# Bounds, orders and the gate tiles' load moved, and every third low part of the gate build given to GpSimd, in a hybrid SSD, attention and PEER block

## The chip, the cores and the metric

The kernel runs on one core of one Trainium2 chip. The metric is the device time of one execution in microseconds (us). The kernel before takes 1569.84 us, the median of three runs (1566.93, 1569.84 and 1572.42). The engines are TensorE (PE; its weight loads are shown as PEld), VectorE (DVE), ScalarE (ACT), GpSimd (POOL) and SyncE (SP, which only issues transfers here).

## The reference

One post-norm layer on x of 512 tokens by 1024, float32, in three parts:

```python
h = layer_norm(x)
proj = h @ w_in                                   # SSM columns | MLA columns
y = concat([ssd(16 heads), mla(8 heads)]) @ w_out # the mixer
h = layer_norm(alpha * h + y)
# PEER: 8 heads, product keys
q = (h @ w_query).reshape(T, 8, 2, 128)
s = einsum('thkd,hknd->thkn', q, sub_keys)
sv, si = top_k(s, 16)                             # per half
top_s, top_pos = top_k(sums of the two halves, 16)
gate = softmax(top_s)                             # expert = i * 128 + j, 16384 experts
act = gelu(einsum('td,thkd->thk', h, u_table[expert]))
ffn = einsum('thk,thkd->td', gate * act, v_table[expert])
out = layer_norm(alpha * h + ffn)
```

## The kernel before, in words

**Stages.** The times in brackets are those of the profiled execution. First come the first layer norm, the projections, the SSM heads and the attention (0 to about 310 us), then the output projection w_out with the second layer norm, block by block of 128 tokens (to about 394). Then comes PEER. The first 384 tokens (NT) are treated densely: the 16384 experts are 128 chunks of 128, and for every chunk the kernel computes act = gelu(U chunk times x) for tokens 0 to 351 (NU); the gates are spread into a dense matrix of expert by token; and the V chunks are multiplied with gate times act and summed up in six PSUM banks (va). Tokens 352 to 383 (UG, 32 of them) get their act from gathered rows of u (`ug_dots`, L1303 to L1321), and the last 128 tokens are done wholly with gathered rows of u and v during the V stage (`gather`).

**U chunks.** A U chunk is 24 matmuls of 128 by 352 (L77 to L79 in `mm3`): high part times high part of x, high times low, low times high, all in f16. `u_halves` (L1519) does one chunk in two halves. The f16 parts come from `Stream`: a raw f32 chunk is loaded by SyncE's queue; `square` (L126) sums its squares on ScalarE; `bound` (L129 to L138) adds these over the partitions with one matmul of 128 by 2 (usq against ones, into any PSUM bank that it is given) and three tiny ScalarE operations make of that a power of two as the scale (us) and its inverse (ui); `his` casts the scaled chunk to f16 on ScalarE (L171); and `splits` makes the low part. On VectorE the low part is one operation with the scale in it (L193, SCALAR_TENSOR_TENSOR, raw times scale less the high part). On GpSimd it is a plain subtraction (L191), and ScalarE first scales the raw chunk in place (L170). Which engine does it is told by `lo_on`: VectorE in routing and in the gate build, GpSimd in the query stage.

**Order.** The program is written out by hand in one order, and each engine runs its own instructions of it strictly in that order. `get` prepares items two ahead; a bound covers two chunks up to chunk 72 (FB), one from there on; `tick` and `bounds` decide by the number of the current chunk which squares and bounds are issued. The 54 first U chunks (LEAD) are spread over the query stage (408 to 517), routing (517 to 565) and the gate build; the others alternate with V chunks in the V stage (from about 760). In the query stage, `w_query_fm` does one query block of 128 columns, `sub_scores` its scores, and `stage1` the top 16 on VectorE. Head 3's result for the last block's tokens is copied to memory by three transfers on ScalarE's queue (r3d). In `routes` VectorE turns positions into expert numbers and ScalarE does the exponential of the softmax.

**Gate build.** `build_g` runs 48 steps. In each, VectorE makes a one-hot of the expert's second digit (`oj`, L1402) and the product of the other digits' one-hots with the gate (`gi`, L1405) for 8 tokens, both f16 with all inputs in SBUF; TensorE multiplies them in 16 small matmuls into two `pw` banks (L1432), ScalarE evicts these to `stg` (L1434), and every fourth step `stg` goes to memory (gs0 for the first two tiles of four chunks, gsp for the others). In the same step there is a dot of one gathered row (L1307 on VectorE; the rows are fetched three ahead by indirect transfers that GpSimd issues, L1301) and about three quarters of a U chunk. `load_g` brings the gates back, four chunks in a tile (gt); the first two are issued on GpSimd's queue (L1651). `v_prep` multiplies them by act (L1677), `v_hi` casts (L1694) and `v_lo` subtracts (L1702). PSUM has four `pw` banks, two `px` and two `pu`; U chunks alternate between the `pu` banks.

**The mixer's end.** The loop over the four blocks b does w_out steps k = 10 to 15 (`w_out_mm`), the layer norm of the block (`ln_mix`) on VectorE with a square root on ScalarE (L252), and `xt_block` (transposes into `px`, evicted as high and low part). Squares of the first four U chunks are made after blocks 0 and 1, and both their bounds after block 2, in one `px` bank; U chunks are let in (`win.on`) after the loop.

## Time and profile before

| | |
|---|---|
| median of three runs | 1569.84 us |
| profiled execution | 1570.85 us |
| its span, first to last instruction | 1569.1 us |
| mean granted TensorE clock | 0.993 |
| busy: PE, DVE, ACT, POOL | 1530.4, 1349.1, 925.3, 499.6 us |
| longest single waits of TensorE after 100 us | 3.3, 3.1, 2.6 and 1.8 us |
| TensorE waits on `gi` in the gate build | 7.8 us in 10 waits |

In the views, a row of the waits reads: engine, its tile and line, `<-` the engine and instruction that released it, then the us in total, the number of times and the longest. A row of the timeline is start, duration, engine, line, operation, tiles (out `<-` in), shapes, count, and in brackets how long the engine had been idle before it and what ended that. Rows with a stretch A:B give its length, then busy us and count of PE, PEld, DVE, ACT and POOL, the granted TensorE clock (1.00 is full speed), the mean DMA share and GB/s. A matmul's shown duration overlaps the next one's, so the time between two starts tells the pace: 0.15 us in a U chunk.

### The profile page before, as it was taken

The numbers are of one execution on the slowest core, as the hardware profiler recorded it, in microseconds if no ns is written. First come the engines' busy times: TensorE is split into PE (matmuls) and PEld (weight loads), VectorE is DVE, ScalarE is ACT, GpSimd is POOL, SyncE is SP. The second block draws the span as 40 slices with busy tenths as digits, with TensorE's granted clock in tenths as the row PEclk, the third lists the DMA queues.
The fourth block names the chain that finished last, engine by engine and source line by source line (L and its number), as shares of the span: only waits on it lengthen the run. The fifth ranks groups of instructions, "written<-read, shape, count | busy, mean of one in ns | idle before, by whom it ended". The sixth has DMA issues, their size and how long they took to land.

```text
span 1569.1 us, 25530 instructions
## 1 busy us (share of the span) xinstructions
PE 1530.4 (98%) x9281; PEld 1167.5 (74%) x9281; DVE 1349.1 (86%) x2609; ACT 925.3 (59%) x1746; POOL 499.6 (32%) x387
## 2 busy tenths in 40 slices
PE   8999999999999999999899999999999999999998
PEld 6787788887677566667677777777777777888886
DVE  8989778746698999999479989999899999999967
ACT  5575566732876788778565565555555554333342
POOL 0000031300144113320033435555555555565400
PEclk9999999999999999999999999999999999999999
DMA  6243123472532469999778899999999999999972
GB/s 253 96 159 99 53 80 91 138 279 71 164 110 93 127 221 353 358 343 295 242 271 330 320 324 330 364 375 371 382 352 391 379 387 325 362 348 367 351 263 92
DMA packets 157888, 404.32 MB, mean 258 GB/s; under 512 B 13801, under 2 KB 66857, under 8 KB 157505
## 3 DMA queue, kind: packets, MB, share of 16 engines
q1 hardware_dynamic: 61072, 212.86, 38.0%
q0 software_dynamic: 45424, 163.73, 28.4%
q10 hardware_dynamic: 51264, 26.09, 5.7%
q8 instruction: 73, 1.20, 0.3%
q14 instruction: 55, 0.44, 0.1%
HBM read 368.33 MB, written 32.19 MB: 255 GB/s over the span
## 4 chain that ended last, share of the span: by engine, by line
PE 78%; DVE 14%; ACT 3%; issue 2%; DMA 1%; ACTq 0%; DVEq 0%
PE va L1710 12%; PE va L1714 11%; PE va L1711 11%; PE pu L77 7%; PE pu L79 7%; PE pu L78 7%; PE pa L77 3%; PE pa L79 3%; PE pa L78 3%; PE pw L1142 3%; DVE gi L1405 2%; DVE wih L193 2%; DVE urow L1307 1%; DVE oj L1402 1%; PE pw L78 1%
## 5 line engine op out<-in xcount | busy, mean ns | idle before, releaser
L1711 PE MATMUL va<-wil,Ph 128*128 128x512 f32 x726 | 283.9, 391 | 0.0
L77 PE MATMUL pu<-XT,wih 128*128 128x352 f16 x896 | 280.8, 313 | 0.0
L79 PE MATMUL pu<-XT,wih 128*128 128x352 f16 x896 | 280.1, 313 | 0.0
L78 PE MATMUL pu<-XT,wih 128*128 128x352 f16 x896 | 280.1, 313 | 0.0
L1775 POOL DMA_INDIRECT row<-u,ix x128 | 169.1, 1321 | 225.5 <-DVE row L1786 130.7
L1775 POOL DMA_INDIRECT row<-v,ix x128 | 182.3, 1424 | 149.5 <-DVE ac L1802 124.1
L176 ACT ACTIVATE wih<-wir 128x1024 fp32r<-128x1024 f32 (+3 forms) x141 | 142.4, 1011 | 120.9 <-PE va L1714 64.6
L198 DVE TENSOR_TENSOR wil<-wir,wih 128x1024 fp32r<-128x1024 f32 (+1 forms) x121 | 147.1, 1217 | 49.0 <-ACT wih L176 42.3
L1710 PE MATMUL va<-wih,Ph 128*128 128x512 f32 x432 | 171.8, 398 | 0.0
L1802 DVE SCALAR_TENSOR_TENSOR ac<-row,hd,ac 128x1024 f32<-128x1024 f32 x128 | 164.0, 1281 | 4.4 <-DMA row<-v,ix 2.1
L1786 DVE SCALAR_TENSOR_TENSOR row<-row,x 128x1024 f32<-128x1024 f32 x128 | 151.5, 1218 | 9.3 <-DMA row<-u,ix 9.2
L1711 PEld LDWEIGHTS va<-wil,Ph 128*128 128x128 f32 x726 | 137.3, 189 | 26.1
L77 PEld LDWEIGHTS <-wih 128*128 128x128 f16 x920 | 89.6, 97 | 61.7 <-issue 19.1
L193 DVE SCALAR_TENSOR_TENSOR wih<-ur,us,wih 128x1024 f16<-128x1024 f32 x97 | 124.2, 1281 | 12.4 <-ACT wih L171 12.4
L1714 PE MATMUL va<-wih,Pl 128*128 128x512 f32 x432 | 133.4, 390 | 0.0
L79 PEld LDWEIGHTS <-wih 128*128 128x128 f16 x920 | 89.8, 98 | 48.7 <-DVE wih L193 1.4
L78 PEld LDWEIGHTS <-wih 128*128 128x128 f16 x920 | 89.9, 98 | 41.1
L1710 PE MATMUL va<-wihx,Ph 128*128 128x512 f32 x294 | 119.0, 405 | 0.7 <-PE pu L132 0.7
L126 ACT ACTIVATE jk<-ur 128x1024 bf16<-128x1024 f32 x114 | 119.2, 1046 | 0.3
L133 ACT ACTIVATE uq<-pu 128x1 uint32<-128x1 uint32 (+1 forms) x81 | 13.7, 169 | 177.7 <-PE pu L132 177.7
L171 ACT ACTIVATE wih<-ur,us 128x1024 f16<-128x1024 f32 x97 | 110.4, 1139 | 2.9 <-ACT stg L1434 2.0
L176 ACT ACTIVATE wihx<-wir 128x1024 fp32r<-128x1024 f32 x50 | 52.9, 1057 | 73.6 <-DMA wir<-v 39.9
(561 smaller groups left out, 3591.1 us busy)
## 6 DMA issues: line engine op xcount, KB each, us to landing
wir<-v SPq DMA_DIRECT2D x128, 512.0 KB, 6.6
ur<-ut SPq DMA_DIRECT2D x105, 512.0 KB, 6.6
gsp<-stg ACTq DMA_DIRECT2D x12, 1920.0 KB, 15.5
gt<-gsp SPq DMA_DIRECT2D x30, 768.0 KB, 8.4
wir<-wo SPq DMA_DIRECT2D x25, 512.0 KB, 4.2
wil<-ut SPq DMA_DIRECT2D x23, 512.0 KB, 4.6
wir<-wf SPq DMA_DIRECT2D x18, 512.0 KB, 3.9
ur<-wqr SPq DMA_DIRECT2D x9, 512.0 KB, 3.6
```

What stands on the lines that cost most here:

```text
L77: T.matmul(ps, lh, rh, start=start, stop=False)
L78: T.matmul(ps, lh, rl, start=False, stop=False)
L79: T.matmul(ps, ll, rh, start=False, stop=stop)
L176: A.activation(h, r, AF.Copy)
L193: V.scalar_tensor_tensor(l, r, self.sc[f][0], h, op0=OP.mult, op1=OP.subtract)
L198: self.lo(n).tensor_tensor(l, r, h, op=OP.subtract)
L1710: T.matmul(va[b][e], Ph[b], h[:, cs], start=c == 0, stop=False)
L1711: T.matmul(va[b][e], Ph[b], l[:, cs], start=False, stop=False)
L1714: T.matmul(va[b][e], Pl[b], h[:, cs], start=False, stop=c == (LASTC if b == 2 and e else 127))
L1775: G.indirect_dma_start(out=R[s], out_offset=None, in_=I["u"] if s < 128 else I["v"], in_offset=bass.IndirectOffsetOnAxis(ap=ix[:, s % 128: ...
L1786: V.scalar_tensor_tensor(r, r, 1.0, x3, op0=OP.mult, op1=OP.mult, accum_out=hd[:, s:s + 1])
L1802: V.scalar_tensor_tensor(ac, r, hd[:, s - 128:s - 127], ac, op0=OP.mult, op1=OP.add)
```

## The change

The change has six parts.

1. `lo_on` becomes a list that is indexed by the item's number. In the gate build it is VectorE, GpSimd, VectorE, so every third U chunk's low part is a GpSimd subtraction and its raw chunk is first scaled in place by ScalarE; twelve low parts move.
2. In the mixer's end, one bound is made after block 1 and one after block 2, each in a `px` bank of its own, ahead of that block's layer norm; U chunks are let in at step (3, 12), where the first one's parts are prepared.
3. In a U chunk the bound stands in the middle (after k = 3) instead of at the end, and its two PSUM columns lie in a `px` bank or in the bank of the chunk before; in a query block it stands after k = 1 with a `pu` bank that the next bounds share.
4. The three r3d transfers are issued at query block 10 instead of right after head 3's top 16.
5. The exponential in `routes` is issued after the copies of the digits and five VectorE operations instead of before.
6. The first two gate tiles' loads are issued before the last half U chunk and the V loads that follow the gate build instead of after them.

```diff
@@ Stream of the weights
-    win = Stream(wst, "wi", items, [128, 1024], raw=3, la=2, lo=lambda n: G if 28 <= n < 48 else lo_on[0])
+    win = Stream(wst, "wi", items, [128, 1024], raw=3, la=2, lo=lambda n: G if 28 <= n < 48 else lo_on[n % len(lo_on)])
@@ w_query_fm
-            win.bounds(win.fi[cnt[0] - 1], lambda: pu()[:, 0:2])
         for k in range(8):
...
+            if k == 1 and m < 16:
+                win.bounds(win.fi[cnt[0] - 1], fresh)
             if k == 2 and m > 0:
                 sub_scores(m - 1)
@@ stage1
         yield top16(rt, sc.pop(m)[:, 0:n], 128, TV4[:, 0:n, m], TI4[:, 0:n, m])
+        if m == 10:
+            f = lambda z: z.rearrange("p h k -> p (h k)")
+            for d, t in zip(r3d, (TS4[:, 3, 0:4], PO4[:, 3, 0:4], TI4[:, 3, 0:8])):
+                nc.scalar.dma_start(d, f(t))
...
                 yield top16(rt, CD.pop(h), 88, TS4[:, 0:n, h], PO4[:, 0:n, h])
-                if h == 3:
-                    f = lambda z: z.rearrange("p h k -> p (h k)")
-                    for d, t in zip(r3d, (TS4[:, 3, 0:4], PO4[:, 3, 0:4], TI4[:, 3, 0:8])):
-                        nc.scalar.dma_start(d, f(t))
@@ routes
         yield 0.6 + n * 0.0025
-        A.activation(f4(d), f4(d), AF.Exp)
         tis(order[0])
...
         V.tensor_tensor(ab(1), v4(pf), v4(b1), op=OP.add)
+        A.activation(f4(d), f4(d), AF.Exp)
         yield 0.8 + n * 0.0042
@@ end of the mixer
             w_out_mm(acc3 if b == 3 else acc, b, k, held[k])
+            if (b, k) == (3, 12):
+                win.on = True
+                win.splits(cnt[0] + 1)
             if (b, k) in XTB:
                 xt_block(XTB[b, k], xm[XTB[b, k]])
...
+        if b in (1, 2):
+            win.bound(px())
         if b < 3:
             xm[b] = ln_mix(b, acc)
...
-        if b == 2:
-            z = px()
-            win.bound(z[:, 0:2])
-            win.bound(z[:, 2:4])
     close(hold)
-    win.on = True
     win.splits(cnt[0] + 2)
@@ before and in u_halves
+    last = []
+
+    def fresh():
+        last[:] = [pu()]
+        return last[0][:, NU:NU + 2]
...
             if k == 3:
                 yield
-        win.bounds(win.fi[cn] + 1, lambda: bank[:, NU:NU + 2] if win.fi[cn] > FB - 5 else pw()[:, 0:2])
+                win.bounds(win.fi[cn] + (win.fi[cn] < 4), lambda: (px() if win.fi[cn] < FB - 4 else last[0])[:, NU:NU + 2])
+        last[0] = bank
...
+    last.append(px())
     u_chunk(0, pw)
@@ around the gate build
+    lo_on[:] = [V, G, V]
     build_g()
-    while half[0] is not None:
-        step_u()
-    win.cap = len(items)
-    win.loads(win.nl + 3)
+    lo_on[:] = [V]
     close(gb, gs[0])
...
     for q in range(2):
         load_g(q)
+    while half[0] is not None:
+        step_u()
+    win.cap = len(items)
+    win.loads(win.nl + 3)
     uc = un[0]
```

How the rows move, at the three places of which the prediction speaks. First ScalarE's queue at the mixer's end (XT are the evictions of `xt_block`, lms is the square root, uq, us and ui belong to a bound, wih at L171 is a high part), before:

```order
L1126 ACTIVATE XT<-px,sxt 128x4x128 x2
L252 ACTIVATE lms<-lmmv,epst 128x1
L133 ACTIVATE uq<-px 128x2
L134 ACTIVATE us<-uq 128x2
L135 ACTIVATE ui<-uq,sxt 128x2
L133 ACTIVATE uq<-px 128x2
L134 ACTIVATE us<-uq 128x2
L135 ACTIVATE ui<-uq,sxt 128x2
L1126 ACTIVATE XT<-px,sxt 128x4x128 x4
L171 ACTIVATE wih<-ur,us 128x1024 x2
```

and in the change:

```order
L1126 ACTIVATE XT<-px,sxt 128x4x128 x2
L133 ACTIVATE uq<-px 128x2
L134 ACTIVATE us<-uq 128x2
L135 ACTIVATE ui<-uq,sxt 128x2
L252 ACTIVATE lms<-lmmv,epst 128x1
L1126 ACTIVATE XT<-px,sxt 128x4x128 x2
L171 ACTIVATE wih<-ur,us 128x1024
L1126 ACTIVATE XT<-px,sxt 128x4x128 x2
L171 ACTIVATE wih<-ur,us 128x1024
```

The bound stands ahead of the square root, and the first high part ahead of block 2's evictions.

Second ScalarE's queue where the V stage begins (act is a U chunk's gelu, Ph the cast of the gates, L176 a V chunk's high part, jk a square), before:

```order
L126 ACTIVATE jk,usq<-ur 128x1024
L133 ACTIVATE uq<-pu 128x1
L134 ACTIVATE us<-uq 128x1
L135 ACTIVATE ui<-uq,sxt 128x1
L1535 ACTIVATE act<-pu,ui 128x352
L1694 ACTIVATE Ph<-gt 128x384 x2
L176 ACTIVATE wih<-wir 128x1024
L126 ACTIVATE jk,usq<-ur 128x1024
L133 ACTIVATE uq<-pu 128x1
```

and in the change:

```order
L126 ACTIVATE jk,usq<-ur 128x1024
L1543 ACTIVATE act<-pu,ui 128x352
L1705 ACTIVATE Ph<-gt 128x384 x2
L176 ACTIVATE wih<-wir 128x1024
L126 ACTIVATE jk,usq<-ur 128x1024
L133 ACTIVATE uq<-pu 128x1
```

A bound now follows its square by one chunk more: the first square's bound stands where the second's stood, and on TensorE that second bound comes in the next chunk.

Third GpSimd's queue in the gate build, where it held the fetches of expert rows alone; piece of the difference:

```order
+L1302 DMA urow<-u,uix 128x1024 x3
+L191 TENSOR_TENSOR wih<-ur,wih 128x1024
+L1302 DMA urow<-u,uix 128x1024 x3
+L191 TENSOR_TENSOR wihx<-wil,wihx 128x1024
+L1302 DMA urow<-u,uix 128x1024 x4
+L191 TENSOR_TENSOR wih<-ur,wih 128x1024
+L1302 DMA urow<-u,uix 128x1024 x4
+L191 TENSOR_TENSOR wih<-ur,wih 128x1024
```

Nine subtractions stand between or right behind the fetches, and three come after them, ahead of the gate tiles' loads.

## The prediction

> **What bounds the kernel now.** I read the engines' totals first, then the busy time in seven stretches cut where the work changes, then the list of what the TensorE queue waited for.
>
> ```profile
> PE 1530.4 (98%) x9281; PEld 1167.5 (74%) x9281; DVE 1349.1 (86%) x2609; ACT 925.3 (59%) x1746; POOL 499.6 (32%) x387
> ```
>
> TensorE is busy 98% of the span, so there are at most 38.7 us to win without removing TensorE work. Where do they lie? In the table by stretch the columns are the stretch, its length, then busy time (and count) of PE, PEld, DVE, ACT and POOL, the granted clock, the DMA share and GB/s.
>
> ```profile
> 0.00:378.00 378.00, 369.44 (x2041) 305.03 (x2042) 291.05 (x555) 212.65 (x411) 47.25 (x42) 1.00 0.40 134
> 378.00:408.00 30.00, 25.37 (x142) 17.80 (x140) 20.54 (x32) 14.88 (x28) 0.00 (x0) 0.94 0.44 140
> 408.00:517.00 109.00, 106.81 (x954) 78.86 (x955) 91.27 (x649) 85.50 (x145) 43.26 (x39) 1.00 0.35 111
> 517.00:565.00 48.00, 44.94 (x288) 28.70 (x287) 47.45 (x82) 37.58 (x76) 8.03 (x9) 0.93 0.53 166
> 565.00:745.00 180.00, 171.57 (x1608) 125.13 (x1607) 177.46 (x245) 147.96 (x296) 44.27 (x32) 1.00 0.97 321
> 745.00:770.00 25.00, 21.02 (x128) 14.61 (x125) 9.63 (x12) 13.55 (x26) 1.11 (x2) 0.86 0.83 258
> 770.00:1569.10 799.10, 791.25 (x4130) 597.36 (x4129) 711.67 (x1039) 413.16 (x767) 355.68 (x264) 1.00 0.89 332
> ```
>
> The first stretch and the V stage (the last row) are TensorE's and the change touches neither. The queries (408 to 517) are TensorE's too. Routing (517 to 565) and the gate build (565 to 745) are VectorE's: 47.45 of 48.00 and 177.46 of 180.00 us busy, while TensorE has 3.1 and 8.4 us to spare. So a cut in TensorE's waiting counts before 517 and after 745, and what happens to VectorE counts between. The waits, in us in total, times, longest:
>
> ```profile
> PE pw L1432 <- DVE gi L1405: 7.8, 10, 1.8
> PE pu L132 <- ACT jk L126: 3.3, 1, 3.3
> PE pu L77 <- ACT act L1535: 3.1, 1, 3.1
> PE px L132 <- ACT uq L133: 2.6, 1, 2.6
> PE px L1156 <- ACT qT L1147: 1.8, 1, 1.8
> PE pw L79 <- DVE wih L193: 0.8, 1, 0.8
> PE va L1710 <- PE pu L132: 0.7, 1, 0.7
> ...
> PE pw L77 <- ACT wih L171: 0.6, 1, 0.6
> ```
>
> Each of the single waits of 1.8 us and more belongs to one edit.
>
> **A, end of the mixer (378 to 394).** The second bound of a pair goes into the bank that ScalarE has yet to read, and ScalarE stands at the square root of the layer norm (L252).
>
> ```profile
> 380.78 0.29 ACT L252 ACTIVATE lms<-lmmv,epst 128x1 f32<-128x1 f32 x1 [4.07 <-DVE lmmv L245]
> 381.18 0.16 PE L132 MATMUL px<-usq,one 128*128 128x2 bf16 x1 [2.58 <-ACT uq L133]
> 382.70:386.10 3.40, 3.40 (x12) 2.71 (x11) 1.27 (x1) 0.00 (x0) 0.00 (x0) 0.50 0.39 142
> ```
>
> The wait is 2.6 us, and the 3.4 us behind it run at half clock, which loses 1.7. The change gives the two bounds banks and places of their own, ahead of that square root, and prepares the first U chunk three w_out steps earlier, so the two waits of that chunk (0.6 and 0.8) go as well: 5.7 in all. About 0.5 comes back, I estimate, since block 3's layer norm still stands behind the second low part on VectorE. I take -5.2; the ends are -2.6 (the wait alone) and -5.7. ScalarE, idle half of this stretch, covers the earlier work.
>
> **B, the queries.** Three copies to memory wait at the head of ScalarE's queue for head 3's result, and the evictions of the next query stand behind them; TensorE's 1.8 us wait is for one of these. In the change they are issued two query blocks later, when that result is long there. -1.8; ends 0 and -1.8. The bounds in this stage change bank and place, and no wait on a bound shows here, so they count nothing.
>
> **C, the exponential.** It is moved behind two copies, so the gelu of a U chunk (3.1 us of waiting) no longer stands behind it. Two half-clock stretches follow that wait:
>
> ```profile
> 526.10:529.50 3.40, 2.56 (x9) 1.32 (x9) 3.33 (x7) 3.39 (x7) 0.00 (x0) 0.50 0.54 182
> 529.50:532.90 3.40, 3.40 (x13) 1.82 (x12) 3.33 (x7) 1.98 (x3) 0.00 (x0) 0.50 0.40 136
> ```
>
> VectorE is busy 3.33 of 3.40 in both: it does not wait for TensorE. The wait is hidden already, so 0; if VectorE were later found waiting, -3.
>
> **D, start of the V stage.** Before, a bound at the end of the last early U chunk waits for a square that ScalarE does behind two casts of the gates.
>
> ```profile
> 759.09 0.31 PE L79 MATMUL pu<-XT,wih 128*128 128x352 f16 x1
> 762.67 0.16 PE L132 MATMUL pu<-usq,one 128*128 128x1 bf16 x1 [3.27 <-ACT jk L126]
> 761.60:765.00 3.40, 1.62 (x5) 1.20 (x5) 2.41 (x4) 3.12 (x8) 0.00 (x0) 0.50 1.15 358
> 765.00:768.40 3.40, 3.40 (x10) 2.63 (x9) 2.25 (x3) 1.39 (x3) 0.00 (x0) 0.50 0.95 295
> 751.93 1.11 POOL L1651 DMA_DIRECT2D gt<-gs  x2 [32.61 <-DVE wil L198]
> 757.97 0.52 DVE L1677 TENSOR_TENSOR gt<-act,gt 128x352 f32<-128x352 f32 x1 [6.54 <-DMA gt<-gs]
> ```
>
> In the change that bound stands in the middle of a chunk and takes the square before. The waits of 3.3 and 0.7 go, and half of the roughly 4.85 us of V matmuls that ran at half clock (2.4): 6.4. Next late is the gate tile: landed at 757.97, then multiply, cast and low part at about 0.55 each, ready near 759.6, just where TensorE now arrives. The load stands ahead of the last U work in the change, so it no longer waits for L198, but the stores that it reads come out of the last gate matmuls, so I count only some tenths, inside the 5.8. On GpSimd's queue it then stands behind the last subtraction, which belongs to an earlier chunk; SP's queue keeps its order. -5.8; ends -3.3 and -6.4.
>
> **E, the gate build.** Twelve low parts move from VectorE to GpSimd; ScalarE does twelve more scalings in place.
>
> ```profile
> L191 POOL TENSOR_TENSOR wih<-ur,wih 128x1024 f16<-128x1024 f32 x9 | 19.2, 2131 | 1.5 <-PE px L1156 1.4
> 675.61 1.28 DVE L193 SCALAR_TENSOR_TENSOR wih<-ur,us,wih 128x1024 f16<-128x1024 f32 x1
> 676.81 0.69 DVE L1402 TENSOR_TENSOR oj<-iotaE,jT 128x1024 f16<-128x1024 f16 x1
> L170 ACT ACTIVATE ur<-ur,us 128x1024 f32<-128x1024 f32 x10 | 11.4, 1139 | 3.8 <-DVE tv L1165 3.8
> ```
>
> VectorE drops 12 times 1.20 us (start to start), 14.4. ScalarE gains 12 x 1.14 = 13.7 on top of 147.96 in 180: it still has some 18 us free. But what does VectorE do while GpSimd subtracts? In the query stage, where GpSimd does these parts now, VectorE runs searches with one input, and they keep their length. Its operations with two inputs from SBUF do not:
>
> ```profile
> 517.27 2.15 POOL L191 TENSOR_TENSOR wih<-ur,wih 128x1024 f16<-128x1024 f32 x1
> 517.25 2.61 DVE L1182 TENSOR_TENSOR cand<-tv 128x48 f32<-128x48 f32 x3
> L1182 DVE TENSOR_TENSOR cand<-tv x6: 220/273/2245, 517.2 to 871.2; 128x48 f32<-128x48 f32 x1, 128x72 f32<-128x72 f32 x1, 128x144 f32<-128x144 f32 x1, 128x64 f32<-128x64 f32 x1
> 299.31 2.54 POOL L198 TENSOR_TENSOR wil<-wir,wih 128x1024 fp32r<-128x1024 f32 x1 [0.87 <-ACT wih L176]
> 301.13 1.79 DVE L198 TENSOR_TENSOR wil<-wir,wih 128x1024 fp32r<-128x1024 f32 x1 [0.66 <-ACT wih L176]
> 303.70 1.23 DVE L198 TENSOR_TENSOR wil<-wir,wih 128x1024 fp32r<-128x1024 f32 x1 [0.17 <-ACT wih L176]
> ```
>
> The small sum at 517.25 took 2.245 us where its fellows take 0.22: it ended 0.08 after GpSimd did. At 301.13 GpSimd had 0.72 left, and VectorE took 0.56 longer than at 303.70. So VectorE stands still for what is left of the GpSimd operation less about 0.2. In the gate build nearly all its operations (the one-hots, their products, the dots, the remaining low parts) have two inputs in SBUF. Twelve stops of 1.9 us less the 1.20 saved are 12 x 0.7 = +8.4. The ends: 12 x (2.13 - 1.20) = +11.2; and if f16 operations, of which none meets GpSimd in this trace, were not stopped, TensorE's 7.8 us of waiting on the products would be all there is to win, -7.8. I take the stop, since every two-input row that meets one shows it.
>
> The Trainium skill, "SBUF — State Buffer", section "Who interferes with whom", says that a VectorE instruction with two SBUF inputs contends with a GpSimd instruction that reads SBUF, and that the later one waits until the first is through, whatever the type. By it alone the part would be +11.2 rather than +8.4; this trace agrees as to the stop, with 2.245 beside 0.22 us.
>
> Two smaller prices. The gather of the 32 rows' experts is issued from the same GpSimd queue:
>
> ```profile
> 671.88 1.74 POOL L1301 DMA_INDIRECT urow<-u,uix  x1 [2.34 <-DVE urow L1307]
> DMA to landing us min/median/max: 4.3/7.3/10.6
> ```
>
> GpSimd has 2.34 us free per step, a subtraction takes 2.13 and may wait for ScalarE's high part; three rows are held at steps of 4.1, so a row has about 3 us more than its 7.3 to land. I take +1.0 for the fetches that come late; ends 0 and +4. And a stop of 1.9 leaves TensorE some 1.5 busy of 3.4, which is what stood ahead of the half clock in A. Four such stretches would cost 6.8 of TensorE time; its room in the stage is 8.4 and grows with E, so +1.4; ends 0 and +3.
>
> The Trainium skill, "TensorE: Matmul & The Clock Gate", section "What's actually happening", has the clock halve only after an idle window of about 3.4 us; by it the 1.4 would fall away and the sum would be 1566.4. The trace speaks against that: 1.5 us idle or so was enough at 381.
>
> **Sum.** The profiled execution took 1570.85 us: its span of 1569.1 and 1.75 around it. -5.2 - 1.8 + 0 - 5.8 + 8.4 + 1.0 + 1.4 = -2.0 gives 1568.85. That execution is 1.0 above the median of 1569.84, so against the median I expect **1568**. With the ends of A to E for this case the own range is 1560 to 1576.
>
> **Rivals.** (1) VectorE's f16 operations are not stopped, and the gate build becomes TensorE's: -5.2 - 1.8 - 5.8 - 7.8 = -20.6, so about 1549. For it: no f16 row contradicts it. Against it: two different f32 operations were stopped, one of them whole, and the stage's DMA share of 0.97 leaves little room to go faster. Chance 0.15.
>
> (2) Slower: GpSimd's queue. Nine of the twelve subtractions stand between gathers of expert rows. Each waits at the head of the queue for ScalarE's high part, itself behind evictions of the gate matmuls. From the point where wait and subtraction exceed the 2.34 us gap and the 3 us of slack together, the row is late and VectorE stands at the dot (L1307), and with it the products. At 1.5 us for each of the nine: +13.5 in place of the +1.0, so 1580. For it: the fetch at 671.88 is issued the moment the dot frees a row, so there is no cushion but the landing time. Against: ScalarE keeps some 18 us free in the stage. Chance 0.17.
>
> (3) The change does not do all it says: the half-clock stretches at A and D come back because the waits are replaced by others (block 3's layer norm at A, the gate tile at D). A and D halve to -5.5: 1573. Chance 0.13.
>
> **How the numbers follow.** The forecast has 0.55. A measurement of this kernel tells some 0.3%, 4.7 us, from no change. Of the 0.55, 0.17 lies below 1565.1, 0.33 within, 0.05 above 1574.5. With rival 1 faster has 0.32; with 0.09 of rival 3 same has 0.42; with rival 2 and the rest of 3 slower has 0.26. The range reaches toward rival 1 and into rival 2: 1553 to 1578.
>
> **What would show it.** The stops: in the gate build, one-hots and products (0.69 and 1.22 us) that take 2 us more wherever an L191 of GpSimd runs, and TensorE's wait on the products at 15 us or more instead of 7.8. A: first U matmul some 4 to 5 us earlier against the last w_out step, granted clock 1.00 from 378 on. B: no 1.8 wait at qT. D: V matmuls directly behind the last early U chunk. Rival 2 would show as VectorE waiting on the fetched rows. If the products keep 1.22 us while GpSimd subtracts, E is wrong by 16 us and the kernel is well below 1560.

## The result, and the profile after

The changed kernel takes 1557.15 us, the median of five runs (1556.80 to 1561.36), against 1569.84 before: a ratio of 0.9924 with a 95% interval of 0.9900 to 0.9948. So it is faster by 0.8%, some 12 us. The forecast was 1568, no change that can be measured.

The profiled execution is the longest of the five: 1561.36 us, span 1559.6. The first view is the busy time by stretch, cut at the same places as for the kernel before (stretch, length, then busy time and count of PE, PEld, DVE, ACT and POOL, granted clock, DMA share, GB/s).

```profile
378.00:408.00 30.00, 28.28 (x187) 20.27 (x186) 22.01 (x33) 18.61 (x33) 0.00 (x0) 1.00 0.54 171
408.00:517.00 109.00, 108.41 (x957) 79.89 (x955) 97.08 (x681) 86.91 (x145) 45.72 (x40) 1.00 0.35 110
517.00:565.00 48.00, 45.42 (x307) 29.36 (x307) 47.48 (x55) 39.01 (x79) 7.66 (x8) 0.96 0.55 180
565.00:745.00 180.00, 164.76 (x1541) 119.57 (x1540) 176.76 (x225) 151.73 (x296) 68.27 (x44) 0.99 0.95 312
745.00:770.00 25.00, 22.98 (x145) 15.88 (x144) 9.98 (x13) 14.90 (x28) 1.75 (x3) 0.93 0.77 248
770.00:1559.60 789.60, 781.78 (x4114) 593.08 (x4112) 709.12 (x1039) 419.97 (x767) 360.31 (x264) 1.00 0.90 337
```

The end of the mixer now runs at full clock (1.00 where it was 0.94). GpSimd does 68.27 us of work in the gate build instead of 44.27, and TensorE gets less done there: 164.76 us instead of 171.57. The waits of TensorE (us in total, times, longest) show the same trade:

```profile
PE pw L1433 <- DVE gi L1406: 15.6, 15, 3.2
PE pb L410 <- DMA XH<-x: 4.5, 1, 4.5
PE va L1721 <- ACT Ph L1705: 2.0, 1, 2.0
PE pu L77 <- ACT act L1543: 1.9, 1, 1.9
...
PE px L132 <- DVE X L1127: 1.0, 1, 1.0
PE px L1123 <- DVE xm L259: 0.7, 1, 0.7
```

The waits of 3.3, 2.6 and 1.8 us are gone; the one on the products has doubled, from 7.8 to 15.6; a new one of 2.0 stands at the first V matmul.

Busy time does not tell where the rest came from. I therefore measured the stages from start to start of the same matmul or product in both traces:

| stretch, us | before | after | difference | predicted |
|---|---|---|---|---|
| start to first query matmul | 406.95 | 402.71 | -4.2 | A: -5.2 |
| first to last query matmul | 101.44 | 98.21 | -3.2 | B: -1.8 |
| last query matmul to first product gi | 59.29 | 59.29 | 0.0 | C: 0 |
| gate build, first to last gi | 174.37 | 182.22 | +7.9 | E: +10.8 |
| last gi to first V matmul | 21.49 | 19.26 | -2.2 | D: -5.8 |
| V stage, first to last matmul of L1710 (L1721 after) | 791.86 | 784.23 | -7.6 | 0 |
| the rest | 13.7 | 13.7 | 0.0 | 0 |

The largest difference is in a row for which nothing was predicted. TensorE is shown busy there for 99% of the time in both traces (791.25 of 799.10 and 781.78 of 789.60 us), so no view of waits or idle time shows it. One change from a U chunk to a V chunk does. Before (start, duration, engine, line; PEld LDWEIGHTS is a weight load):

```profile
1007.84 0.31 PE L79 MATMUL pu<-XT,wih 128*128 128x352 f16 x1
...
1007.99 0.17 PE L132 MATMUL pu<-usq,one 128*128 128x1 bf16 x1
1007.99 0.19 PEld L1710 LDWEIGHTS va<-wih,Ph 128*128 128x128 f32 x1
1008.01 0.48 PE L1710 MATMUL va<-wih,Ph 128*128 128x512 f32 x1
...
1008.10 0.19 PEld L1711 LDWEIGHTS va<-wil,Ph 128*128 128x128 f32 x1
...
1008.33 0.39 PE L1711 MATMUL va<-wil,Ph 128*128 128x512 f32 x1
```

And after, at the same kind of place:

```profile
1010.09 0.31 PE L79 MATMUL pu<-XT,wih 128*128 128x352 f16 x1
1010.09 0.19 PEld L1721 LDWEIGHTS va<-wihx,Ph 128*128 128x128 f32 x1
1010.12 0.51 PE L1721 MATMUL va<-wihx,Ph 128*128 128x512 f32 x1
...
1010.47 0.40 PE L1722 MATMUL va<-wil,Ph 128*128 128x512 f32 x1
```

From the start of the last U matmul to the start of the second V matmul it is 0.49 us before (1007.84 to 1008.33) and 0.38 after. Before, 71 of the 74 changes have the bound there; 70 of them take 0.49 us (the first of all has a wait), and the three without a bound take 0.38 already in that trace. After, 73 take 0.38. The rows suggest a reason. Before, the f32 weights of the first V matmul begin to load with the bound (L132), a matmul of 0.03 us, and the next load follows only 0.11 us later (1007.99 to 1008.10), so part of the load sticks out behind the bound. Now it begins with a U matmul of 352 columns, which covers it: 0.38 is the 0.15 of a U matmul and the 0.23 at which V matmuls follow each other. That was the reason to be tested first.

### The profile page after: what moved, and what is told of

Its sections match the earlier page's. It is cut to its first block, busy times and chain, and to the rows that moved or that the text cites. A ratio compares the mean times of both kernels' runs of the same rounds, so it can differ in the third digit from the quotient of the medians.

```text
span 1559.6 us, 25551 instructions
## 1 busy us (share of the span) xinstructions
PE 1521.3 (98%) x9281; PEld 1162.9 (75%) x9281; DVE 1353.4 (87%) x2597; ACT 944.6 (61%) x1758; POOL 531.2 (34%) x399
## 4 chain that ended last, share of the span: by engine, by line
PE 83%; DVE 11%; ACT 3%; issue 2%; DMA 1%; DVEq 0%; ACTq 0%; POOLq 0%
PE va L1721 11%; PE va L1722 11%; PE va L1725 11%; PE pu L77 8%; PE pu L79 8%; PE pu L78 8%; PE pw L1141 5%; PE pa L77 3%; PE pa L79 3%; PE pa L78 3%; DVE gi L1406 2%; DVE urow L1308 2%; DVE oj L1403 1%; DVE wih L193 1%; PE pw L77 1%
## 5 line engine op out<-in xcount | busy, mean ns | idle before, releaser
L79 PE MATMUL pu<-XT,wih 128*128 128x352 f16 x896 | 280.6, 313 | 0.0
L1786 POOL DMA_INDIRECT row<-u,ix x128 | 173.5, 1355 | 212.9 <-DVE row L1797 122.9
L176 ACT ACTIVATE wih<-wir 128x1024 fp32r<-128x1024 f32 (+3 forms) x141 | 142.5, 1011 | 137.1 <-PE va L1725 79.9
L1721 PE MATMUL va<-wih,Ph 128*128 128x512 f32 x432 | 172.8, 400 | 0.0
L1543 ACT ACTIVATE act<-pu,ui 128x352 f32<-128x352 f32 x124 | 68.5, 553 | 105.2 <-PE pu L79 103.3
L79 PEld LDWEIGHTS <-wih 128*128 128x128 f16 x920 | 90.0, 98 | 48.1 <-DVE wih L193 0.5
L193 DVE SCALAR_TENSOR_TENSOR wih<-ur,us,wih 128x1024 f16<-128x1024 f32 x92 | 118.0, 1283 | 7.8 <-ACT wih L171 7.7
L1721 PE MATMUL va<-wihx,Ph 128*128 128x512 f32 x294 | 119.8, 408 | 2.0 <-ACT Ph L1705 2.0
L171 ACT ACTIVATE wih<-ur,us 128x1024 f16<-128x1024 f32 x92 | 104.9, 1140 | 3.1 <-ACT stg L1435 1.9
L176 ACT ACTIVATE wihx<-wir 128x1024 fp32r<-128x1024 f32 x50 | 52.8, 1057 | 80.6 <-PE va L1725 41.7
```

The costliest lines, as they stand in the source:

```text
L79: T.matmul(ps, ll, rh, start=False, stop=stop)
L176: A.activation(h, r, AF.Copy)
L193: V.scalar_tensor_tensor(l, r, self.sc[f][0], h, op0=OP.mult, op1=OP.subtract)
L1721: T.matmul(va[b][e], Ph[b], h[:, cs], start=c == 0, stop=False)
L1786: G.indirect_dma_start(out=R[s], out_offset=None, in_=I["u"] if s < 128 else I["v"], in_offset=bass.IndirectOffsetOnAxis(ap=ix[:, s % 128: ...
```

## The experiments

All times are medians; the ratios are to the kernel before on the same chip, whose own median was between 1567.9 and 1572.7 in these comparisons. The stages are those of the table above, each from the profiled execution.

| kernel | us | ratio (95%) | first query | queries | gate build | to V | V stage |
|---|---|---|---|---|---|---|---|
| before | 1569.84 | | 406.95 | 101.4 | 174.4 | 21.5 | 791.9 |
| changed | 1557.15 | 0.9924 (0.9900-0.9948) | 402.71 | 98.2 | 182.2 | 19.3 | 784.2 |
| before, bound in mid-chunk | 1560.24 | 0.9945 (0.9926-0.9964) | 406.99 | 101.2 | 174.4 | 17.1 | 782.6 |
| bound behind part 7 | 1559.01 | 0.9939 (0.9918-0.9960) | 402.80 | 98.3 | 182.4 | 18.3 | 783.6 |
| bound behind part 8 | 1564.73 | 0.9978 (0.9964-0.9991) | 402.75 | 98.4 | 181.5 | 17.1 | 789.7 |
| no low part moved | 1553.61 | 0.9899 (0.9877-0.9922) | 402.66 | 98.4 | 174.6 | 20.1 | 784.3 |
| two of three moved | 1570.31 | 0.9989 (0.9972-1.0006) | 402.58 | 98.2 | 191.3 | 20.1 | 784.3 |
| mixer undone | 1562.22 | 0.9940 (0.9923-0.9958) | 406.42 | 98.2 | 182.5 | 17.5 | 782.7 |
| copies, exponential undone | 1560.97 | 0.9930 (0.9906-0.9954) | 402.59 | 102.0 | 181.5 | 17.0 | 782.6 |
| query bounds undone | 1557.11 | 0.9907 (0.9873-0.9941) | 402.53 | 98.3 | 182.0 | 17.0 | 783.3 |
| gate load undone | 1556.83 | 0.9910 (0.9875-0.9946) | 402.67 | 98.3 | 181.5 | 17.0 | 782.6 |
| late store | 1558.29 | 0.9917 (0.9889-0.9946) | 402.67 | 98.5 | 181.9 | 17.0 | 782.6 |
| none moved, late store | 1552.03 | 0.9880 (0.9850-0.9909) | 402.70 | 98.2 | 174.2 | 19.2 | 782.6 |
| none moved, store first | 1550.56 | 0.9865 (0.9841-0.9889) | 402.65 | 98.3 | 175.5 | 17.1 | 782.6 |

### The V stage: where the bound stands

Three kernels. The first is the kernel before with the bound moved in the V stage alone:

```diff
             if k == 3:
                 yield
+                if c >= LEAD:
+                    win.bounds(win.fi[cn], lambda: last[0][:, NU:NU + 2])
+        last[:] = [bank]
+        if c < LEAD:
-        win.bounds(win.fi[cn] + 1, ...)
+            win.bounds(win.fi[cn] + 1, ...)
```

> The kernel before, with one part of the change alone: in the V stage the small bound matmul (L132, 128x1) stands in the middle of each U chunk and not at its end, where the next matmul loads f32 weights. Theory (a matmul of some 0.03 us is too short to hide a weight load of 0.19 us behind it; one of 352 columns is not): 74 changes from U to V, each 0.11 us shorter, so the V stage goes from 791.9 to about 784 us and the whole from 1569.8 to about 1562. Rival (the V stage became shorter for another reason: a neater start, fewer stretches of half clock, other times of the gates' loads): less than 3 us, 1567 to 1570.

The V stage shrank to 782.6 us and the whole by 7.6 (1567.88 to 1560.24 on that chip). That goes with the theory. But 9.2 us in the V stage is more than 8, and "to V" shrank too, since the first chunk of the V stage also lost its wait for the square. So the place itself had to be separated from what else it moves. The two others are the changed kernel with the bound behind the seventh or the eighth part of a U chunk, 0.45 us apart:

```diff
             if k == 3:
                 yield
+            if k == (6 if c >= LEAD else 3):      # the other kernel: 7
                 win.bounds(...)
```

> The changed kernel, where in the V stage the bound matmul stands behind the seventh of the eight parts of a U chunk instead of the fourth, so 1.35 us later but still ahead of matmuls with f16 weights (loads of 0.10 us). Theory of the weight load: nothing changes, V stage 784 +- 1 us, whole 1557 +- 2. Rival (what counts is how early ScalarE gets its scales): a good part of the 7.6 us is lost, V stage 787 to 792, whole 1560 to 1565.

> The changed kernel, where in the V stage the bound matmul stands behind the last part of a U chunk, so directly ahead of the V matmuls with their f32 weights; only 0.45 us later than in the kernel with the seventh part. Theory of the weight load: 74 times 0.11, V stage 792, whole 1565. Rival (how early ScalarE gets its scales): hardly different from the kernel with the seventh part.

Behind part 7 the V stage is 783.6 us, behind part 8 it is 789.7: 6.15 us for a move of 0.45 us (whole: 5.7, on the same chip). How early ScalarE gets its scales is thereby excluded as the main cause, since 1.35 us more of delay, from part 4 to part 7, cost 1.0 us at most (783.6 beside 782.6); what follows the bound decides. In the kernel with part 8 the old pattern is back:

```profile
1008.82 0.31 PE L79 MATMUL pu<-XT,wih 128*128 128x352 f16 x1
1008.97 0.17 PE L132 MATMUL pu<-usq,one 128*128 128x1 bf16 x1
1009.00 0.47 PE L1722 MATMUL va<-wihx,Ph 128*128 128x512 f32 x1
1009.31 0.39 PE L1723 MATMUL va<-wil,Ph 128*128 128x512 f32 x1
```

0.49 us again from L79 to the second V matmul. In mid-chunk, ahead of f16 weights, the bound costs its own 0.03 us and no more, here in the changed kernel:

```profile
1000.71 0.17 PE L132 MATMUL pu<-usq,one 128*128 128x1 bf16 x1
1000.74 0.31 PE L77 MATMUL pu<-XT,wih 128*128 128x352 f16 x1
```

My 74 x 0.11 = 8.1 was too high, as these 0.03 us are still paid. The price is read best from the start of one U chunk to the start of the next, with a V chunk between (medians): 7.813 us in the kernel before and behind part 8, 7.727 behind part 7, 7.713 in the changed kernel. So the pair differs by 0.086 us at each of 71 places, 6.1 in all, as it measured, and the move of the change is worth 0.100 at each, 7.1 us in all. Why part 7 costs 0.014 more than part 4 stays open. The shortest V stage of all runs, in six of them, is 782.6. The kernel before lies 9.2 above it: 7.1 from the bound, and about 2.1 from the V matmuls at its start that ran at half clock (4.9 us of them). No run changed the type of the V weights, so the place of the bound is shown as the cause, and the exposed weight load is the reading that fits the rows.

The Trainium skill, "TensorE: Matmul & The Clock Gate", section "Back-to-back issue gap", says that the spacing of matmuls is set by the matmul and the weight load together, and gives a floor of about 25 ns for up to 64 columns; the bound's 0.028 us (median of 70 in the changed kernel) agrees. Its section "Weight-path perf modes" has the fast weight load on only for weights that are not f32; the loads here, 0.10 us for f16 and 0.19 for f32, agree with that too.

### The gate build: how many low parts move

```diff
-    lo_on[:] = [V, G, V]
```

> The changed kernel with all 36 low parts of the gate build on VectorE again; everything else as changed. Theory (twelve stops of VectorE of 1.94 us less 1.20 us saved each): the gate build, first to last product gi, shrinks from 182.2 us back to about 174.4, TensorE's wait on the products from 15.6 back to about 8, and the whole is 8 us faster than the changed kernel: about 1549 against 1557. Rival (the gate build is paced by what it loads, or by the slots of TensorE, so that the stops lie beside other work): no more than 3 us faster, 1554 to 1557. Rival (the moved low parts help, and the stage is longer for another reason): 1557 or more.

The gate build went back to 174.6 us, 7.65 less, and TensorE's wait on the products to 10.0. The profiled executions differ by 6.55 (1561.36 and 1554.81), because the start of the V stage was 0.9 worse in this one and the query stage 0.2 longer. The medians differ by less (ratios 0.9899 and 0.9924, so 3.9 us), and the intervals of the two ratios overlap; the section on the gate tile gives the likely reason. The stage is what shows that the moved low parts cost time. The whole agrees: without them the runs took 1550.54 to 1555.29, and on the same chip the kernel with the bound behind part 7, which has them, took 1557.57 to 1561.03. The stops that the prediction named are there. GpSimd's subtraction and what VectorE had then, in the changed kernel:

```profile
563.02 2.20 POOL L191 TENSOR_TENSOR wih<-ur,wih 128x1024 f16<-128x1024 f32 x1 [15.95 <-ACT wih L171]
563.15 3.15 DVE L1406 TENSOR_TENSOR gi<-dhi,dgl 128x2048 f16<-128x2048 f16 x1
...
596.17 1.22 DVE L1406 TENSOR_TENSOR gi<-dhi,dgl 128x2048 f16<-128x2048 f16 x1
...
597.09 2.29 POOL L191 TENSOR_TENSOR wih<-ur,wih 128x1024 f16<-128x1024 f32 x1
597.31 3.15 DVE L1308 SCALAR_TENSOR_TENSOR urow<-urow,ux 128x1024 f32<-128x1024 f32 x1
```

A product in f16 takes 3.15 us under a subtraction and 1.22 beside none; so does a dot. By groups (count, busy us, mean ns):

```profile
L1406 DVE TENSOR_TENSOR gi<-dhi,dgl 128x2048 f16<-128x2048 f16 x48 | 60.2, 1255 | 0.0
L1308 DVE SCALAR_TENSOR_TENSOR urow<-urow,ux 128x1024 f32<-128x1024 f32 x32 | 52.4, 1639 | 0.2 <-DMA urow<-u,uix 0.2
L1403 DVE TENSOR_TENSOR oj<-iotaE,jT 128x1024 f16<-128x1024 f16 x48 | 35.8, 745 | 1.2 <-PE px L132 1.2
```

The dots rose from 39.0 to 52.4 us, gi from 58.4 to 60.2, oj from 32.8 to 35.8, and dgl, another product of two inputs in SBUF, by 2.6: 20.8 us of stops for 14.4 saved, 6.4 net. Ten of the twelve subtractions stopped a VectorE operation for about 2 us (seven dots, one each of gi, oj and dgl). Beside the last two, at 727.54 and 742.60, VectorE lost 0.7 us and nothing, and the subtractions themselves took 4.10 and 3.05 us instead of 2.13, so there GpSimd seems to be the one that waited. VectorE waited 0.2 us for fetched rows (1.1 with no part moved): GpSimd's queue delayed nobody.

The other way, two of three:

```diff
-    lo_on[:] = [V, G, V]
+    lo_on[:] = [V, G, G]
```

> The changed kernel with two of every three low parts of the gate build on GpSimd (24 instead of 12). Theory (each moved part stops VectorE by 1.94 us and saves 1.20; with 12 of them the gate build was 7.65 us longer than with none, 0.64 each): gate build 182.2 + 12 x 0.64 = 189.9 us, whole about 7.7 us above the changed kernel, 1565. Rival (GpSimd's queue: with 24 subtractions of 2.13 us between 32 gathers of rows the rows come late and VectorE stands at the dots for them): more than in proportion, gate build 194 us or more, whole 1569 or more, and waits of the dots on the fetched rows of 3 us and more in all.

The gate build took 191.3 us, 9.1 more for twelve more parts, 0.76 each where the first twelve cost 0.64: a little above proportion, not the 194 of the rival, whose sign is missing as well: VectorE waited 0.6 us in all for fetched rows.

The whole, 1570.31, lies where the rival put it, but not by the rival's mechanism. The profiled execution is 9.8 us above that of the changed kernel, 9.1 of it in this stage; against the median it is 13; its profiled execution has the late gate tile (below), and so, I suppose, have its other runs (1567.60 to 1571.57). What makes the price rise from 0.64 to 0.76 I did not settle; four stretches at half clock in the stage, where the changed kernel had one, are a candidate.

### Mixer, queries, routing

```diff
-            if (b, k) == (3, 12):
-                win.on = True
-                win.splits(cnt[0] + 1)
...
-        if b in (1, 2):
-            win.bound(px())
...
+        if b == 2:
+            z = px()
+            win.bound(z[:, 0:2])
+            win.bound(z[:, 2:4])
     close(hold)
+    win.on = True
```

> The changed kernel with the end of the mixer undone: the two pairs of bounds both behind block 2, and the first U chunk prepared where it was. Theory: the wait of 2.6 us behind ScalarE's square root comes back, with a stretch at half clock (1.7) and the first chunk's waits on its parts (0.6 + 0.8), so the first query matmul comes at about 406.5 instead of 402.7; the first query chunk waits 0.7 for its low part again; in all +4.3 to +5, whole about 1562. Rival (layer norm of block 3 sets the end of this stage in any case): 402.7 to 404, whole +1 or less.

The first query matmul came at 406.42, 3.7 later, with the old waits of 2.6, 0.6 and 0.8. The stretch at half clock did not come back with them: the clock was 1.00 from 382.7 to 386.1, where the kernel before has 0.50. The wait of 1.0 on X stayed. That is A, undone. The query stage stayed at 98.2: the 0.7 us of the first query chunk did not come back. A is smaller than predicted because two waits took the place of the old ones (px L132 on X, 1.0, and px L1123 on xm, 0.7, in the list of the changed kernel), both behind the layer norm of block 3.

```diff
-        if m == 10:
-            ... the three copies of head 3
...
+                if h == 3:
+                    ... the three copies of head 3
...
+        A.activation(f4(d), f4(d), AF.Exp)
         tis(order[0])
...
-        A.activation(f4(d), f4(d), AF.Exp)
```

> The changed kernel with two parts undone: the three copies of head 3 stand at their old place on ScalarE's queue, and the exponential ahead of the two copies. Theory: the copies bring back the wait of 1.8 us at qT, query stage from 98.2 to about 100.2 us; the exponential does nothing, since VectorE paces the routing: 59.3 us from the last query matmul to the first product as before; whole 2 us above the changed kernel. Rival (the exponential counts): routing 3 us longer, whole +5.

The query stage grew by 3.8 us, to 102.0, twice what was expected. The wait at qT is 1.9; the other half is a stretch at half clock behind it:

```profile
477.40:480.80 3.40, 1.48 (x14) 1.07 (x13) 1.78 (x13) 2.96 (x8) 2.13 (x2) 1.00 0.17 37
480.80:484.20 3.40, 3.40 (x18) 2.18 (x17) 3.40 (x27) 2.90 (x5) 0.00 (x0) 0.51 0.39 141
```

TensorE was busy 1.48 of 3.40 us, and the next 3.40 ran at half clock. The kernel before has the same wait without such a stretch. Routing took 59.26 us, so the exponential is worth nothing.

```diff
             ps = pw()
+            win.bounds(win.fi[cnt[0] - 1], lambda: pu()[:, 0:2])
...
-            if k == 1 and m < 16:
-                win.bounds(win.fi[cnt[0] - 1], fresh)
```

> The changed kernel with the bounds of the query stage ahead of each query chunk again, in a bank of their own, as before the change. The query stage went from 101.4 to 98.2 us, of which the copies' wait explains 1.8. Theory (the other 1.4 us come from the bounds' place): query stage 99.2 to 99.8 us, a wait of the first query chunk on its low part (0.7) again, whole +1 to +1.5. Rival (the 1.4 us have another origin, the end of the mixer or the queue ahead): 98.2 us as in the changed kernel.

98.3 us: the rival was right, the bounds' place alone does not bring the 1.4 us. Most of them, 1.2, are the two first query chunks of the kernel before (6.16 and 6.48 us from start to start; 5.24 and 6.21 after), and 0.7 of that is a wait of the first chunk for its low part on VectorE (L193), which the changed kernel does not have. The chunk with the wait at qT makes up the rest: it was longer by 2.05 us (8.26 and 6.21), not by 1.8. Neither the old mixer alone nor the old bounds alone brings the 1.2 us back; whether both together do was not tried, and it stays open.

### The gate tile

```diff
+    while half[0] is not None: ...          # the last early U work and its loads
     close(gb, gs[0])
...
     for q in range(2):
         load_g(q)
-    while half[0] is not None: ...
```

> The changed kernel with the load of the first two gate tiles behind the last early U work again. Theory 1 (the load waits for the store it reads, not for its place in the order, and the wait of 3.3 us was removed by moving the bound alone): from the last product gi to the first V matmul 17 to 20 us as in the runs so far (19.3, 20.1, 18.3, 17.1), whole within 1.5 us of the changed kernel. Theory 2 (the order is what brings the tile in time): the load is issued behind a cast some 2 to 4 us later, the first V matmul comes 2 to 4 us later, with a stretch at half clock behind it, whole +3 to +6.

17.0 us to the first V matmul, better than the changed kernel's 19.3, and 1556.83 in all: theory 1, the place of the load in the order is worth nothing that shows. But then what makes 17 or 20? I suspected the last store of the gates (1920 KB), which is issued close to the tile's load:

```diff
         uc += 1
-        if rest:
-            rest.pop()()
+    while rest:
+        rest.pop()()
     close(gs[1])
```

> The changed kernel with that store alone moved. Theory: last product to first V matmul about 17 us, whole 1554 to 1556. Rival: 18 to 19.5 us, whole 1557 to 1558.

> The changed kernel with all low parts of the gate build on VectorE, and with the last store of the gates (1920 KB, which is read only later) issued behind the last early U chunk and not between the store and the load of the first gate tile. Theory (in the runs so far the tile's load took 4.5 to 5.9 us where it was issued ahead of that store and 6.5 to 8.8 us beside it): load landed 4.5 to 6 us after its issue, no wait of TensorE for the high part of the gates, last product gi to first V matmul 17 to 17.7 us instead of 20.1, no half clock behind it; whole 3 to 4 us below the kernel with the low parts on VectorE alone: about 1550. Rival (the load is slow because of the other loads, or of the store ahead of it): 18.5 to 20 us as before, whole 1553.

The first gave 17.0, but 1558.29 in all. The second, which has all low parts on VectorE as well, issued the store 3.6 us behind the tile's load and still had 19.2 us, with 7.3 us from the tile's load to the multiplication. So that store is not the cause. All profiled executions together point to another. The columns are the issue of the next U chunk's load (512 KB, SyncE's queue) relative to the issue of the tile's store (128 KB); the time from that store to the tile's load, which waits for it; from the end of that load's issue (0.57 us) to the multiplication; and from the last gi to the first V matmul.

| kernel | U load against store | store to load | load to multiply | to V |
|---|---|---|---|---|
| before | -0.37 | 4.4 | 5.5 | 21.5 |
| changed | -0.08 | 4.6 | 7.6 | 19.3 |
| no low part moved | -0.17 | 4.7 | 8.3 | 20.1 |
| bound behind part 7 | -0.23 | 4.6 | 6.5 | 18.3 |
| mixer undone | -0.28 | 4.4 | 5.9 | 17.5 |
| none moved, late store | -0.24 | 4.7 | 7.3 | 19.2 |
| before, bound in mid-chunk | +0.34 | 2.4 | 5.3 | 17.1 |
| bound behind part 8 | +0.26 | 2.5 | 4.5 | 17.1 |
| copies, exponential undone | +0.32 | 2.4 | 4.5 | 17.0 |
| gate load undone | +0.34 | 2.5 | 5.0 | 17.0 |
| late store | +0.21 | 2.5 | 4.5 | 17.0 |
| query bounds undone | +0.34 | 2.5 | 4.5 | 17.0 |
| two of three moved | +5.75 | 2.5 | 8.4 | 20.1 |

Wherever the U load went first, by 0.1 to 0.4 us, the tile's load was issued 2 us later, and it then came beside other transfers. (In the last row the 1920 KB store was issued 0.5 us ahead of the tile's load, and two loads of 512 KB some 3 us behind it.) To see whether this is cause or company, the store was put on SyncE's queue ahead of that U load, with the low parts on VectorE and the tile's load behind the early U work again:

```diff
-    lo_on[:] = [V, G, V]
...
-                nc.scalar.dma_start(gs0[...], qv(stg[:, 0:8]))
+                first = lambda e, ...: e.dma_start(gs0[...], qv(s))
+                first(nc.scalar) if n < 47 else rest0.append(first)
...
-    for q in range(2):
-        load_g(q)
...
     win.loads(win.nl + 3)
+    rest0.pop()(nc.sync)
+    for q in range(2):
+        load_g(q)
```

> The changed kernel with all low parts of the gate build on VectorE, and the last store of the first gate tiles on SP's queue directly ahead of the next load of a U chunk (512 KB). In the eleven runs with the store on ScalarE's queue, the store took 4.4 to 4.7 us wherever that U load was issued 0.1 to 0.3 us ahead of it, and 2.4 to 2.5 us wherever it was issued behind it (or not at all near it). Theory (the transfer that is issued first is through first): store 2.5 us, load of the gate tile issued 7.8 to 8.2 us after the last product gi, landed some 5 us later, last product to first V matmul 17.0 us instead of 20.1, no half clock behind it (V stage 782.6 instead of 784.3): 4.7 us less than the profiled execution with the low parts on VectorE alone, about 1550 against its 1554.8. Rival (the two only happen together, both being late or early by the clock of the loads): store 4.5 us, 19 to 20 us to the first V matmul, 1552 to 1555.

(There were thirteen such executions, with those of the two kernels compared.) In the changed kernel, times from the start (SPq and ACTq are transfers issued on SyncE's and ScalarE's queues):

```profile
747.73 0.33 SPq L116 DMA_DIRECT2D ur<-ut  x1
747.80 0.38 ACTq L1439 DMA_DIRECT2D gs<-stg  x1
...
751.73 0.33 SPq L105 DMA_DIRECT2D wir<-v  x1
...
752.41 1.10 POOL L1658 DMA_DIRECT2D gt<-gs  x2 [6.76 <-DMA gs<-stg]
...
760.56 0.53 DVE L1688 TENSOR_TENSOR gt<-act,gt 128x352 f32<-128x352 f32 x1 [8.86 <-DMA gt<-gs]
```

And with the store first:

```profile
741.27 0.38 SPq L1439 DMA_DIRECT2D gs<-stg  x1
...
741.75 0.67 SPq L116 DMA_DIRECT2D ur<-ut  x1
...
743.87 1.11 POOL L1662 DMA_DIRECT2D gt<-gs  x2 [30.81 <-DMA gs<-stg]
...
745.20 0.33 SPq L105 DMA_DIRECT2D wir<-v  x1
...
750.57 0.53 DVE L1693 TENSOR_TENSOR gt<-act,gt 128x352 f32<-128x352 f32 x1 [5.40 <-DMA gt<-gs]
```

From the store to the tile's load it takes 2.6 us instead of 4.6, the load is issued ahead of the V chunk's load (wir) instead of behind it, 17.1 us to the first V matmul, no half clock there, V stage 782.6. The theory held: both stages came out as it said to a tenth of a microsecond. This run changed the store's queue together with the order, so which of the two is needed is not separated; in the table, where the store always stands on ScalarE's queue, the order alone goes with the 2 us from store to load. The profiled execution is 3.9 us below that with the tile late and not 4.7, because the gate build was 1.0 longer (175.5), which I did not follow up. This kernel has the lowest median of all: 1550.56, 0.9865 of the kernel before, and 6.6 us below the changed kernel. From the two others with no low part moved it cannot be told apart by the whole time, as the intervals overlap; the two stages tell them apart.

The same would explain the medians. The changed kernel's profiled execution has the late tile; with 17.0 to V and 782.6 in the V stage it would take 3.9 us less, 1557.5, which lies among its four other runs (1556.80 to 1557.79). The kernel with no low part moved has two runs near 1550.5, three near 1554.8, the profiled one being of the latter, and one between. This is an inference: the other executions have no trace.

## Why the prediction was right or wrong

The sum was -2.0 against the profiled execution; it measured -9.5. The time lies inside the range given, but 11 us under the forecast. That it lies inside is partly luck: the range reached down to 1553 for rival 1, which did not happen, and the own range ended at 1560. (Nor does that own range follow from the ends named: taken together, without VectorE going unstopped, they give 1561 to 1582.)

**The step that failed** is in the reading of the bound: "The first stretch and the V stage (the last row) are TensorE's and the change touches neither", which puts the V stage at 0. The change does touch it: the bound moves in every U chunk there, and that is worth 7.1 us by the pace of the chunks, nearly all of the 7.6 that the stage gained. The bounds of the query stage were left out with a reason, "no wait on a bound shows here, so they count nothing"; the V stage shows that a bound can cost time where no wait shows. A stretch with TensorE busy all the time was taken for one that cannot get faster without less work. The trace before had the difference: 0.49 us at 70 changes from U to V, and 0.38 at the three without a bound.

**E, the gate build: mechanism right, size a third too high.** Twelve stops at +8.4 net; the trace has ten whole ones and a part, 20.8 - 14.4 = 6.4, and the stage +7.9 (+7.65 by the undoing); the 1.5 between was not traced. The +1.0 for late fetches was 0.2 us of waiting. The +1.4 for half clock cannot be seen: one such stretch appeared (683.5), and TensorE has time to spare in the stage. The rule that VectorE stands still for f16 operations too, on which rival 1 hung, held: gi at 3.15 us instead of 1.22. TensorE's wait on the products came out at 15.6 us, the sign named.

The Trainium skill, "SBUF — State Buffer", section "Who interferes with whom", had this: two SBUF inputs on VectorE against a read of GpSimd, with no condition on the type. These traces agree, f16 included (1.22 to 3.15 us).

**A: right, 1.0 too large.** The clock is 1.00 from 378 to 408, the first U matmul came 4.8 us earlier (393.72 to 388.94), but the first query matmul only 4.2 (3.7 by the undoing), since block 3's layer norm then gives waits of 1.0 and 0.7 where I had set 0.5. The 1.7 for half clock hangs on the execution: with the old waits put back, the clock stayed at 1.00. And the row at 381 is misread where E uses it a second time: 1.5 us is what TensorE was busy ahead of that half clock; it was idle for 1.9.

**B: right in place, too small.** -1.8 was the wait; the stage gained 3.2. The wait can also carry a stretch at half clock, as the undoing showed. Of the other 1.4 us, 1.2 lie in the first two query chunks; 0.7 of them is the wait for a low part, and why it went is not settled.

**C: right.** 59.29 us before and after.

**D: named rightly what is late next, then counted it as in time.** "Next late is the gate tile ... ready near 759.6, just where TensorE now arrives": it was ready at 761.7, and the wait of 2.0 with a stretch at half clock behind it left -2.2 to the first V matmul, and about half a microsecond of half clock, of the -5.8. This is the half of rival 3 that came true; in executions where the store goes first, the gain is 4.5 to the first V matmul and some 2.1 of half clock, more than was forecast. I had held the order of the load for worth some tenths; it is worth nothing that shows. What goes with the delay is 0.1 us on another queue.

**Rivals.** 1 fell with the stops; 2 fell with 0.2 us of waiting for rows; of 3 the half at D came, the half at A did not.

## What to carry to other kernels

Where an engine is shown busy throughout, measure from start to start across each change of work: a tiny matmul ahead of one with f32 weights cost 0.1 us more than in mid-chunk, at 71 places, and showed in no list of waits. Work that is moved to GpSimd has to be priced with the operations of VectorE that it will stop, not with the time that it frees. Where a small store gates a critical load, put it ahead of the large transfer of the other queue in one and the same queue, as in the last kernel here, instead of leaving it to a tenth of a microsecond.

## What was unexpected in the hardware

- The weight load of an f32 matmul took 0.19 us and of an f16 one 0.10; behind a matmul of one column the f32 load was exposed in part (0.11 us from its start to that of the next load), behind one of 352 columns it was not (0.38 us, as the paces of the matmuls alone give).
- Of two transfers issued 0.1 to 0.5 us apart, the order mattered: the load that waits for the store of 128 KB came 2.4 to 2.6 us after the store where this was ahead of a load of 512 KB, and 4.4 to 4.7 where it was behind it. Two traces have the landings: before, with the load first by 0.37 us, both took 3.8 us to land; with the store first, the store took 1.9 and the load 4.0. The Trainium skill, "DMA: Bandwidth & Descriptors", section "Issuing engines are not separate DMA queues", has the transfers of all issuing engines run on the same 16 DMA engines and interleave; the shared engines fit this, but with an interleaving of equals the 0.1 us would not matter as much as it did.
- Apart from the start and the very end of an execution, half clock followed on 3.4 us in which TensorE was still busy, by its recorded matmuls, for 0.2 to 1.5 us, never on a whole idle stretch. In the changed kernel:

```profile
680.10:683.50 3.40, 1.30 (x20) 1.30 (x21) 3.40 (x6) 0.63 (x2) 0.01 (x1) 1.00 1.09 350
683.50:686.90 3.40, 3.40 (x15) 1.75 (x13) 3.40 (x5) 3.03 (x7) 1.62 (x2) 0.51 1.09 358
```

  The stretches come and go between kernels with the same wait: the 2.6 us at the mixer's end brought half clock in the kernel before and none with the mixer undone, and a wait of 1.8 to 1.9 us at qT cost 2.05 us in one kernel and 3.8 in another.
